# Final sums of a diffusion-block kernel: x1 of two token tiles through an identity product, all by halves of 512 columns, the last norm's weights loaded during the experts

## The chip, the cores and the metric

The kernel runs on one core of a Trainium2 chip, in one launch. The metric is the device time of one execution in microseconds; of several runs the median is taken. TensorE (PE) multiplies, VectorE (DVE) and ScalarE (ACT) work on tiles, GpSimd (POOL) does small vector steps and issues indirect and other DMAs, SyncE (SP) issues most of the weight DMAs.

## The reference, cut to what matters

The reference is one layer of a hybrid block (attention and a gated recurrence side by side), then a mixture of experts, then a final norm, over 512 tokens of 1024 channels:

```python
x = x + mod_lat[2] * mix_lat                       # x1 below
h_lat = rmsnorm(x, norm_ffn_g[l]) * (1 + mod_lat[4]) + mod_lat[3]
x = x + mod_lat[5] * moe_ffn(h_lat, ...)           # top 4 of 32 experts, D_EXPERT = 1024
return rmsnorm(x, final_norm_g)

def rmsnorm(x, g):
    y = x * rsqrt(mean(x * x, axis=-1, keepdims=True) + EPS)
    return y * g
```

An expert is an up product of 1024 by 2048 (gate and linear part interleaved), a clamped SwiGLU, and a down product of 1024 by 1024; each token's four expert outputs are weighted by a softmax of the router's four best values.

## The kernel before, in words

**Tokens.** The 512 tokens are four tiles of 128 rows. After the mixers, x1 (the stream after the first residual) lies in DRAM in three pieces `x1p`, of columns 0 to 511, 512 to 767 and 768 to 1023.

**Experts.** The 32 experts run one after the other, sorted so that the largest come first. Their weights come in chunks of 1 MB: eight of `w_gu` and four of `w_dn` each. `load_chunk` (L818) issues them from SyncE into 16 slots, through `next_chunk` (L1219), which gives back the slot of the chunk before and loads the next ones into free slots. `up` (L1257) multiplies the gathered rows of an expert with eight chunks, `glu` does the activation, `turned_acts` (L1278) transposes it, `down` (L1296) multiplies with four chunks, which this document calls its quarters, and scales the sums by the token's probability and the modulation `m5` into `yt` (L1305). `scatter` (L1309) adds `yt` to x1 in DRAM with indirect DMAs from POOL, for experts 0 to 30.

**The last expert.** Expert 31 is not scattered. Its rows in `yt` (64 slots, columns 0 to 511 on partitions 0 to 63, columns 512 to 1023 on partitions 64 to 127) are put in the place of their tokens by a product with a one-hot matrix `oh` of tokens by slots: for each token tile t two products (L1394), one per half of the columns, into PSUM. DVE adds the 1024 columns of PSUM to x1 of the tile (L1396). Then `finish_tile` (L1373) takes the sum of squares on ACT (Square with an accumulator, L1375; the profile shows the read of the accumulator as an instruction of its own), the reciprocal root on POOL (two steps, L125 and L126), scales by it and by the last norm's weights `gain` on DVE (L1377), and writes the tile out, tiles 0 to 2 from ACT's queue, tile 3 from SyncE's (L1378).

**What is loaded for the end.** After the last up product is in the program, `hold` takes five of the slots that were used last and are free: the first for `gain` (1024 weights, the same on all 128 partitions, loaded by SyncE at L1388), the others for x1 of tiles 0 to 3. `load_x2` (L1367) loads x1 from DRAM with twelve DMAs from POOL, three per tile, behind the scatters of expert 30. A slot that served the chunk k of the last up product can be written when that chunk's products are done: with five in `hold`, `gain` has chunk 6 and the tiles 0 to 3 chunks 5, 4, 3 and 2.

**PSUM.** There are eight banks of 512 columns: "gu" and "dn" are one tile each of three banks, "tp" is two tiles of one bank. Token tiles 0 and 2 use "gu", 1 and 3 use "dn"; a tile may be written when its last reader is done.

**Order.** The functions write a program order. A planner then orders the instructions of each engine: it follows a cost model and takes, of those whose inputs it believes to be ready, the one that is earliest in the program; instructions inside `tc.high_priority()` go ahead. It also sets every wait. Each engine then works through its queue in that order. The pool `y2k` has 18 buffers of 512 columns: during the experts they hold the transposed inputs and activations, three for `m5`, and short-lived tables.

**After the tiles.** From L1400 all engines load a count of experts with too many tokens. It is zero here, so the loop that would handle them, and finish the tiles again, is passed over.

Of the kernel before, what the change touches and what calls it, by code (L numbers as in the profile page):

```python
# [11 lines left out]
F32 = mybir.dt.float32  # L12
# [5 lines left out]
AF = mybir.ActivationFunctionType  # L18
OP = mybir.AluOpType
# [4 lines left out]
D = 1024  # L24
S = 512
# [3 lines left out]
NE = 32  # L29
# [17 lines left out]
NR = 3  # L47
# [32 lines left out]
def tile_block(ctx: ExitStack, tc: tile.TileContext, x, xc, cols, w_mod, b_mod, w_in, w_q_b, w_kv_b,  # L80
               w_out, g_ffn, w_r, b_r, w_gu, b_gu, w_dn, b_dn, g_fin, cst, rope, msk, out):
    nc = tc.nc
    V, A, G, PE, SP = nc.vector, nc.scalar, nc.gpsimd, nc.tensor, nc.sync
# [9 lines left out]
    ident = cs[:, K_ID:K_ID + 128]  # L93
# [22 lines left out]
    def y2k(dt, nm):  # L116
        return ypool.tile([128, S], dt, name=nm, tag="y2k")
# [55 lines left out]
    with tc.tile_pool(name="pa", bufs=1) as pa:  # L173
# [17 lines left out]
        for i in range(6):  # L191
            t = pa.tile([128, D], F32, name="xt", bufs=4)
            src = x[i * 128:(i + 1) * 128] if i < 4 else xc[(i - 4) * 128:(i - 3) * 128]
# [20 lines left out]
        for i in range(6):  # L214
            sq = pa.tile([128, D], BF16, name="sq")
# [3 lines left out]
            p = wide().rearrange("p a (k t) -> p (a k) t", t=128)  # L219
# [10 lines left out]
        for g in range(2):  # L230
            for which in (1, 0):

                pm = bank()[:, :128]
                for k in range(KD):
                    w = wms[8 * g + 4 * (1 - which) + k // 2]
                    for j in range(4):
                        PE.matmul(pm[32 * j:32 * j + 32], sc32[:, k], w[:, k % 2, j * 128:(j + 1) * 128],
                                  start=k == 0, stop=k == KD - 1)
# [9 lines left out]
                if which == 1:  # L248
                    gm = col[:, C_GM + 4 * g:C_GM + 4 * g + 4]
                    V.scalar_tensor_tensor(dst, dst, 1.0, gm[:, :, None].broadcast_to([128, 4, 2]),  # L250
                                           op0=OP.add, op1=OP.mult)
            for k in range(4 * g, 4 * g + 4):
                hf = pa.tile([128, T], F32, name="hf", bufs=2)
                for j, (a, b) in enumerate(((0, S), (S, T))):
                    V.tensor_scalar(hf[:, a:b], xnT[:, k, a:b], ac[:, k, j:j + 1], bc[:, k, j:j + 1],
                                    op0=OP.mult, op1=OP.add)
# [541 lines left out]
    def buffer(i, dt=F32):  # L798
        return pools[i].tile([128, 2 * D], dt, name=f"slot{i}")
# [72 lines left out]
    with tc.tile_pool(name="wo", bufs=2, side="right") as wo:  # L872
# [10 lines left out]
        for k in range(3, KD):  # L883
            t = buffer(k - 3, F32R).rearrange("p (a d) -> p a d", a=2)
            load_wo(k, t[:, 0], t[:, 1])
        rstack.close()
        early = ctx.enter_context(tc.tile_pool(name="sle", bufs=1))
# [204 lines left out]
    yt = piece(F32, 2)  # L1092
    glus = [piece(F32, i)[:, :NR * 256] for i in (3, 4)]

    free = deque(range(14, N_BUF))

    def borrow(dt=F32):

        i = free.popleft()
        free.append(i)  # L1100
        return buffer(i, dt)

    with tc.tile_pool(name="mo", bufs=2) as mo, tc.tile_pool(name="eps", bufs=2, space=PSUM) as eps:
# [115 lines left out]
        def next_chunk(key):  # L1219

            free.extend(taken)
            i, raw = raws.pop(key)
            taken[:] = [i]
            while n_loaded[0] < len(chunks) and free:
                load_chunk(free.popleft())
            return raw
# [66 lines left out]
                    V.tensor_copy(aT[1][:, 2:, b:b + 32], p[:, 2 * r:2 * r + 2, 96:])  # L1293
            return aT

        def down(e):  # L1296
            ps = sums(e, "dn")
            bias(ps, e, 256, 2 * D)
            for q in range(4):
                raw = next_chunk((e, "dn", q))  # L1300
                for j in range(2):
                    product(ps, e, aTs[e][q // 2][:, 2 * (q % 2) + j], raw[:, j * D:(j + 1) * D], 256, q + j == 4)
            big = CAPS[e] == CAP
            for r in rounds(e):
                V.scalar_tensor_tensor(yt[:, 256 * r:256 * r + 256], ps[:, r, :256],  # L1305
                                       prob[:, e, r * big:r * big + 1], (m5x if big else m5y)[r],
                                       op0=OP.mult, op1=OP.mult)
# [18 lines left out]
        for r in range(NR):  # L1326
            G.tensor_copy(m5x[r][:96], m5[:96, 256 * r:256 * r + 256])
            G.tensor_copy(m5x[r][96:], m5[96:, 768:])
        m5c = y2k(F32, "m5")
        m5y = [m5c[:, :256], m5c[:, 256:]]  # L1330
        for r in range(2):
# [24 lines left out]
                xTs[e + 1] = turned(xgs[(e + 1) % 2], CAPS[e + 1])  # L1356


        hold = [free.pop() for _ in range(5)]
        gain, xs = buffer(hold[0])[:, :D], []  # L1360

        def weighed(y, ps, pb):
            for n in range(2):
# [2 lines left out]

        def load_x2():  # L1367
            for t in range(4):
                xs.append(buffer(hold[1 + t])[:, :D])
                for a, b, x1 in x1p:  # L1370
                    G.dma_start(xs[t][:, a:b], x1[t * 128:(t + 1) * 128])

        def finish_tile(t, u):  # L1373
            sm = mo.tile([128, 4], F32, name="sm", bufs=4)
            A.activation(borrow()[:, :D], u, AF.Square, accum_out=sm[:, 0:1])  # L1375
            r = rstd_small(sm[:, 2:3], sm[:, 0:1], D, 1)
            v = V.scalar_tensor_tensor(u, u, sm[:, 2:3], gain, op0=OP.mult, op1=OP.mult).ins  # L1377
            o = (SP if t == 3 else A).dma_start(out[t * 128:(t + 1) * 128], u).ins  # L1378
            return r, v, o


# [3 lines left out]
            V.tensor_scalar(gf[:, t], gidx[:, NE - 1, 0:1], -128.0 * t, None, op0=OP.add)  # L1385
        V.tensor_tensor(oh, iota[:, None, :].broadcast_to([128, 4, 128]), gf.broadcast_to([128, 4, 128]), OP.is_equal)

        SP.dma_start(gain, bass.AP(tensor=g_fin.tensor, offset=g_fin.offset, ap=[[0, 128], [1, D]]))  # L1388
        load_x2()
        down(NE - 1)  # L1390
        for t in range(4):
            p = eps.tile([128, NR, S], F32, name=("gu", "dn")[t % 2], bufs=1)[:, :2]
            for n in range(2):
                PE.matmul(p[:, n], oh[64 * n:64 * n + 64, t], yt[64 * n:64 * n + 64, :S], start=True, stop=True)  # L1394
            with tc.high_priority():
                V.tensor_tensor(xs[t], xs[t], p.rearrange("p a b -> p (a b)"), OP.add)  # L1396
                last = finish_tile(t, xs[t])


        with tc.issue_after(last[0]), tc.issue_after(last[1]), tc.issue_after(last[2]):  # L1400
# [2 lines left out]
        with tc.For_i(0, n_any):  # L1403
            with tc.For_i(0, n_ov) as i:
                ev = nc.values_load(ov_e[0:1, ds(i, 1)], min_val=0, max_val=NE - 1)
                ex = nc.values_load(ov_x[0:1, ds(i, 1)], min_val=0, max_val=NE - 1)
                rk = mo.tile([128, 4, 1], F32, name="rk", bufs=1)
                V.tensor_tensor(rk, rankm[:, :, ds(ev, 1)], ov_r[:, None, ds(i, 1)].broadcast_to([128, 4, 1]), OP.subtract)
                pe = mo.tile([128, 4, 128], BF16, name="pe", bufs=1)
                V.tensor_tensor(pe, iota[:, None, :].broadcast_to([128, 4, 128]), rk.broadcast_to([128, 4, 128]),  # L1410
                                OP.is_equal)
                inf = mo.tile([128, 4, 8], BF16, name="inf", bufs=1)
                V.tensor_scalar(inf[:, :, None], info[:, :, ds(ev, 1), :], 1.0, None, op0=OP.mult)
                ps = eps.tile([128, 4, 128], F32, name="tp").rearrange("p a b -> p (a b)")
                for t in range(4):
                    PE.matmul(ps[:, :8], pe[:, t], inf[:, t], start=t == 0, stop=t == 3)
                gi = mo.tile([128, 1], I32, name="gi", bufs=1)
                pb = mo.tile([128, 1], F32, name="pb", bufs=1)
                slot_tables(mo, ps[:, :8], 1, gi, pb)
                selc = mo.tile([96, 128], BF16, name="selc", bufs=1)  # L1420
                V.tensor_scalar(selc, sel[:, ds(ev, 1)].to_broadcast([96, 128]), 1.0, None, op0=OP.mult)
                xg = xgs[0]
                gather(xg, gi)

                def in_turn(src):
                    h = y2k(F32, "oT")
                    p = eps.tile([128, 4, 128], F32, name="tp").rearrange("p a b -> p (a b)")
                    for k in range(4):
                        PE.transpose(p[:, k * 128:(k + 1) * 128], src[:, k * 128:(k + 1) * 128], ident)
                    V.tensor_copy(h, p)  # L1430
                    return h.rearrange("p (k s) -> p k s", s=128)

                def layer(ps, part, xT, w):
                    for n in range(2):
                        c0 = part * D + n * S
                        PE.matmul(ps[:, n], selc, bias_t[:, c0:c0 + S], start=True, stop=False)
                    for c in range(KD):
                        raw = borrow()[:, :D]
                        SP.dma_start(raw, w(c))
                        for n in range(2):  # L1440
                            PE.matmul(ps[:, n], xT[c // 4][:, c % 4], raw[:, n * S:(n + 1) * S],
                                      start=False, stop=c == KD - 1)

                xT = [in_turn(xg[:, a * S:(a + 1) * S]) for a in range(2)]
                aT = []
                for n in range(2):
                    ps = eps.tile([128, NR, S], F32, name="gu", bufs=1)[:, :2]
                    layer(ps, n, xT, lambda c: w_gu[ds(ex, 1), c * 128:(c + 1) * 128, n * D:(n + 1) * D]
                          .rearrange("e r c -> (e r) c"))
                    aT.append(in_turn(glu(ps, *(z[:, :S] for z in glus))))  # L1450
                ps = eps.tile([128, NR, S], F32, name="dn", bufs=1)[:, :2]
                layer(ps, 2, aT, lambda c: w_dn[ds(ex, 1), c * 128:(c + 1) * 128].rearrange("e r c -> (e r) c"))
                y = borrow()[:, :D]
                weighed(y, ps, pb)
                for a, b, x1 in x1p:
                    add_rows(x1, y[:, a:b], gi)
            scatter(NE - 1)
            del xs[:]
            load_x2()
            for t in range(4):  # L1460
                finish_tile(t, xs[t])


# [58 lines left out]
```

## Time and profile before

| | us |
|---|---|
| median of the runs shown | 1993.99 (1990.43, 1993.99, 1994.44) |
| profiled execution | 1993.45 |
| its span | 1991.5 |
| PE busy | 1855.6 (93%) |
| DVE busy | 816.8 (41%) |
| ACT busy | 430.4 (22%) |
| POOL busy | 277.8 (14%) |
| HBM read | 495.95 MB, 258 GB/s over the span |

The span is the time between the first and the last instruction of the profiled execution; all positions in this document are microseconds from its start. TensorE's granted clock is 0.986 of full speed over the span. The experts take about the second half, from 913 on, where the DMA engines move near 400 GB/s. The part that the change touches is the last 60 us, and one load early in the experts.

### The profile page before, as it was taken

The numbers are of one execution on the slowest core, as the hardware profiler recorded it, in microseconds if no ns is written. First come the engines' busy times: TensorE is split into PE (matmuls) and PEld (weight loads), VectorE is DVE, ScalarE is ACT, GpSimd is POOL, SyncE is SP. The second block draws the span as 40 slices with busy tenths as digits, with TensorE's granted clock in tenths as the row PEclk, the third lists the DMA queues.
The fourth block names the chain that finished last, engine by engine and source line by source line (L and its number), as shares of the span: only waits on it lengthen the run. The fifth ranks groups of instructions, "written<-read, shape, count | busy, mean of one in ns | idle before, by whom it ended". The sixth has DMA issues, their size and how long they took to land.

```text
span 1991.5 us, 40184 instructions
## 1 busy us (share of the span) xinstructions
PE 1855.6 (93%) x17276; PEld 1176.4 (59%) x17276; DVE 816.8 (41%) x1449; ACT 430.4 (22%) x717; POOL 277.8 (14%) x266
## 2 busy tenths in 40 slices
PE   5999999999999999998999999998899899988984
PEld 4999988998888788884355443333343334333431
DVE  5477877786757677755121111101110111010102
ACT  4233333333334554521000000000000000000001
POOL 1023000000000000012121221211221121212122
PEclk8999999999999999998999999999999999999998
DMA  9312434343121111369999999999999999999994
GB/s 301 98 56 84 137 118 121 99 140 85 33 77 55 44 38 53 91 259 371 346 396 395 394 404 391 393 398 406 388 399 398 399 388 396 394 403 386 402 402 160
DMA packets 164609, 512.68 MB, mean 257 GB/s; under 512 B 18640, under 2 KB 96370, under 8 KB 115276
## 3 DMA queue, kind: packets, MB, share of 16 engines
q1 hardware_dynamic: 149996, 487.99, 64.8%
q0 software_dynamic: 13856, 19.99, 4.4%
q8 instruction: 137, 2.24, 0.5%
q10 hardware_dynamic: 576, 2.10, 0.3%
q14 instruction: 44, 0.36, 0.1%
HBM read 495.95 MB, written 17.12 MB: 258 GB/s over the span
## 4 chain that ended last, share of the span: by engine, by line
PE 66%; DMA 28%; DVE 2%; issue 1%; ACT 1%; POOL 0%; SPq 0%; DVEq 0%; ACTq 0%; POOLq 0%
PE sc L282 24%; DMA slot<-in_w_gu 14%; PE gu L1255 14%; DMA slot<-in_w_dn 12%; PE dn L1255 7%; PE sc L688 3%; PE acc L434 3%; PE tp L709 1%; PE tp L1285 1%; PE sc L934 1%; PE acc L282 1%; PE sc L935 1%; PE sc L936 1%; DMA raw<-in_w_mod 1%; PE tp L1214 1%
## 5 line engine op out<-in xcount | busy, mean ns | idle before, releaser
L1255 PE MATMUL gu<-slot,xT 128*32 128x512 f32 x5120 | 579.2, 598 | 42.7 <-DMA slot<-in_w_gu 41.9
L282 PE MATMUL sc<-hh,part 128*128 128x384 f32 (+1 forms) x1472 | 404.6, 370 | 3.0 <-ACT part L120 3.0
L1255 PEld LDWEIGHTS gu<-slot,xT 128*32 128x32 f32 x5120 | 174.0, 110 | 391.3 <-issue 294.2
L1255 PE MATMUL dn<-slot,aT 128*32 128x256 f32 x5120 | 301.3, 382 | 10.9 <-DMA slot<-in_w_dn 10.1
L282 PEld LDWEIGHTS sc<-hh,part 128*128 128x128 f32 x1472 | 269.2, 190 | 34.6 <-issue 6.6
L1255 PEld LDWEIGHTS dn<-slot,aT 128*32 128x32 f32 x5120 | 157.0, 110 | 131.0 <-DMA slot<-in_w_dn 19.5
L1271 DVE TENSOR_SCALAR part<-gu 128x768 f32<-128x768 f32 (+1 forms) x32 | 26.4, 825 | 506.4 <-PE gu L1255 506.4
L282 PE MATMUL sc<-hl,part 128*128 128x384 f32 (+1 forms) x736 | 233.4, 365 | 0.0
L1274 ACT ACTIVATE part<-part 128x768 f32<-128x768 f32 (+1 forms) x32 | 23.6, 737 | 707.1 <-DVE part L1271 707.1
L1202 POOL DMA_INDIRECT x1d<-part,gidq x48 | 63.7, 1328 | 579.0 <-DVE part L1305 422.1
L282 PEld LDWEIGHTS sc<-hl,part 128*128 128x128 f32 x736 | 136.7, 189 | 11.2 <-issue 0.2
L121 DVE TENSOR_TENSOR part<-raw,part 128x1024 fp32r<-128x1024 f32 (+1 forms) x101 | 102.7, 1019 | 93.4 <-ACT part L120 93.3
L120 ACT ACTIVATE part<-raw 128x1024 fp32r<-128x1024 f32 (+1 forms) x101 | 89.4, 888 | 204.2 <-PE sc L282 146.8
L1305 DVE SCALAR_TENSOR_TENSOR part<-dn,prob,m 128x256 f32<-128x256 f32 x80 | 34.4, 479 | 237.4 <-PE dn L1255 224.8
L1202 POOL DMA_INDIRECT x1d<-part,gidx x77 | 108.3, 1407 | 86.3 <-DVE part L1305 60.4
L434 PE MATMUL acc<-qq,kc 128*128 128x128 f32 x448 | 63.4, 285 | 0.5 <-DVE qq L451 0.5
L434 PEld LDWEIGHTS acc<-qq,kc 128*128 128x128 f32 x448 | 60.9, 191 | 3.2 <-DVE qq L451 1.0
L430 ACT ACTIVATE kc<-kk 128x512 f32<-128x512 f32 x56 | 37.8, 675 | 108.8 <-PE acc L434 76.1
L441 DVE TENSOR_TENSOR kk<-kk,tt 128x768 f32<-128x768 f32 x56 | 59.0, 1054 | 0.0
L852 DVE TENSOR_TENSOR pe<-cs,rankm 128x384 bf16<-128x384 f32 x32 | 17.7, 553 | 98.6 <-PE tp L863 95.2
L451 DVE TENSOR_TENSOR qq<-qq,tt 128x256 f32<-128x256 f32 x112 | 47.2, 463 | 21.2 <-PE acc L434 21.0
L1196 POOL DMA_INDIRECT part<-h2d,gidx x31 | 32.3, 1042 | 161.5 <-PE tp L1214 125.2
(365 smaller groups left out, 2102.9 us busy)
## 6 DMA issues: line engine op xcount, KB each, us to landing
slot<-in_w_gu SPq DMA_DIRECT2D x256, 1024.0 KB
slot<-in_w_dn SPq DMA_DIRECT2D x128, 1024.0 KB
raw<-in_w_in SPq DMA_DIRECT2D x64, 512.0 KB
raw<-in_w_mod SPq DMA_DIRECT2D x48, 512.0 KB
raw<-in_w_q_b SPq DMA_DIRECT2D x12, 384.0 KB
xt<-in_x SPq DMA_DIRECT2D x8, 512.0 KB
raw<-in_w_out SPq DMA_DIRECT2D x8, 512.0 KB
raw<-in_w_kv_b SPq DMA_DIRECT2D x16, 128.0 KB
```

Source lines behind the costliest of these rows:

```text
L120: A.activation(hi, src, AF.Copy)
L121: V.tensor_tensor(lo, src, hi.bitcast(F32), OP.subtract)
L282: PE.matmul(ps[:, j, :b - a], w, x[:, a:b], start=first and n == 0, stop=last and n == 2)
L430: A.activation(kc, comb(kk, T, b, S), AF.Copy)
L434: PE.matmul(p[:, c], kc[:, c * 128:(c + 1) * 128], comb(qq, S, b, 128, c * 128), start=True, stop=True)
L441: V.tensor_tensor(kv_, kv_, mu, OP.mult)
L451: V.tensor_tensor(qv, qv, fv.broadcast_to([128, nb, b]), OP.mult)
L688: PE.matmul(ps[:, i, :HT], lhs, rhs[:, a:e], start=n == 0, stop=n == 4)
L1196: G.indirect_dma_start(out=xg, out_offset=None, in_=h2d, in_offset=bass.IndirectOffsetOnAxis(ap=idx, axis=0), bounds_check=S - 1, oob_is_e ...
L1202: G.indirect_dma_start(out=x1, out_offset=bass.IndirectOffsetOnAxis(ap=idx, axis=0), in_=y, in_offset=None, bounds_check=S - 1, oob_is_err ...
L1255: PE.matmul(ps[rows, r, :w], xT[:, slots], wt[:, cols_], start=False, stop=last)
L1305: V.scalar_tensor_tensor(yt[:, 256 * r:256 * r + 256], ps[:, r, :256], prob[:, e, r * big:r * big + 1], (m5x if big else m5y)[r], op0=OP.m ...
```

## The change

`down` gets a parameter `between`, a function that is called ahead of the products of the last quarter; for the last expert it is `early`. `early` writes, for tiles 0 and 1, a product of the identity with each half of the tile's x1 into PSUM (`begin`), as the first of two accumulating products; the one-hot product then adds to it, so that the sum of these tiles stands in PSUM and DVE's addition falls away. Tile 0 uses two banks of "gu", tile 1 the two "tp" tiles, tile 2 "dn" and tile 3 "gu". For tiles 2 and 3 DVE adds as before, by halves.

`finish_tile` works by halves of 512 columns: two Squares with two accumulators, an addition of them on POOL (one more step), the two steps of the root as before, and two scalings, from PSUM into the tile's buffer for tiles 0 and 1, in place for 2 and 3. The tile is written out with one DMA as before.

`gain` is two `y2k` buffers, loaded by POOL with two DMAs of 512 columns at the start of the experts, between the copies of `m5`; SyncE's load at the end falls away. `hold` is four slots: x1 of tiles 0 to 3 has the slots of chunks 6, 5, 4 and 3.

```diff
-        def down(e):
+        def down(e, between=None):
             ps = sums(e, "dn")
             bias(ps, e, 256, 2 * D)
             for q in range(4):
                 raw = next_chunk((e, "dn", q))
+                if between and q == 3:
+                    between()
                 for j in range(2):
...
+        gain = [y2k(F32, "gain") for _ in range(2)]
+        for n in range(2):
+            G.dma_start(gain[n], bass.AP(tensor=g_fin.tensor, offset=g_fin.offset + n * S, ap=[[0, 128], [1, S]]))
...
-        hold = [free.pop() for _ in range(5)]
-        gain, xs = buffer(hold[0])[:, :D], []
+        hold, xs = [free.pop() for _ in range(4)], []
...
-                xs.append(buffer(hold[1 + t])[:, :D])
+                xs.append(buffer(hold[t])[:, :D])
...
-        def finish_tile(t, u):
+        def column_halves(a):
+            return [a[:, n * S:(n + 1) * S] for n in range(2)]
+
+        def finish_tile(t, src):
             sm = mo.tile([128, 4], F32, name="sm", bufs=4)
-            A.activation(borrow()[:, :D], u, AF.Square, accum_out=sm[:, 0:1])
+            sq, u = column_halves(borrow()), column_halves(xs[t])
+            for n in range(2):
+                A.activation(sq[n], src[n], AF.Square, accum_out=sm[:, n:n + 1])
+            G.tensor_tensor(sm[:, 0:1], sm[:, 0:1], sm[:, 1:2], OP.add)
             r = rstd_small(sm[:, 2:3], sm[:, 0:1], D, 1)
-            v = V.scalar_tensor_tensor(u, u, sm[:, 2:3], gain, op0=OP.mult, op1=OP.mult).ins
-            o = (SP if t == 3 else A).dma_start(out[t * 128:(t + 1) * 128], u).ins
+            for n in range(2):
+                v = V.scalar_tensor_tensor(u[n], src[n], sm[:, 2:3], gain[n], op0=OP.mult, op1=OP.mult).ins
+            o = (SP if t == 3 else A).dma_start(out[t * 128:(t + 1) * 128], xs[t]).ins
             return r, v, o
...
-        SP.dma_start(gain, bass.AP(tensor=g_fin.tensor, offset=g_fin.offset, ap=[[0, 128], [1, D]]))
         load_x2()
-        down(NE - 1)
+        ends = {}
+
+        def begin(t):
+            if t == 1:
+                ends[t] = [eps.tile([128, 4, 128], F32, name="tp").rearrange("p a b -> p (a b)") for _ in range(2)]
+            else:
+                p = eps.tile([128, NR, S], F32, name="dn" if t == 2 else "gu", bufs=1)
+                ends[t] = [p[:, n] for n in range(2)]
+            for n, x1 in enumerate(column_halves(xs[t])):
+                if t < 2:
+                    PE.matmul(ends[t][n], ident, x1, start=True, stop=False)
+
+        def early():
+            begin(0)
+            begin(1)
+
+        down(NE - 1, early)
         for t in range(4):
-            p = eps.tile([128, NR, S], F32, name=("gu", "dn")[t % 2], bufs=1)[:, :2]
+            if t > 1:
+                begin(t)
             for n in range(2):
-                PE.matmul(p[:, n], oh[64 * n:64 * n + 64, t], yt[64 * n:64 * n + 64, :S], start=True, stop=True)
+                PE.matmul(ends[t][n], oh[64 * n:64 * n + 64, t], yt[64 * n:64 * n + 64, :S], start=t > 1, stop=True)
             with tc.high_priority():
-                V.tensor_tensor(xs[t], xs[t], p.rearrange("p a b -> p (a b)"), OP.add)
-                last = finish_tile(t, xs[t])
+                src = ends[t]
+                if t > 1:
+                    src = column_halves(xs[t])
+                    for n in range(2):
+                        V.tensor_tensor(src[n], src[n], ends[t][n], OP.add)
+                last = finish_tile(t, src)
```

## Rows read from the trace of the kernel before

**Rows 1.** Chain of waits in order of time, tail: start us, us, what.

```profile
1940.23 25.17 DMA slot<-in_w_dn
...
1965.44 1.98 PE dn L1255 x32
...
1968.47 1.14 PE gu L1394 x4
...
1969.63 1.23 DVE slot L1396
...
1980.52 1.28 DVE slot L1377
```

**Rows 2.** Timeline of TensorE: start us, us, what, [idle before <- releaser].

```profile
1955.54 0.74 PE L1285 MATMUL tp<-cs,part 128*128 128x128 f32 x4 [2.22 <-DVE part L1275]
...
1962.05 1.93 PE L1255 MATMUL dn<-slot,aT 128*32 128x256 f32 x32 [1.52 <-DMA slot<-in_w_dn]
1965.44 1.93 PE L1255 MATMUL dn<-slot,aT 128*32 128x256 f32 x32 [1.46 <-DMA slot<-in_w_dn]
...
1969.40 1.05 PE L1394 MATMUL dn<-part,oh 64*128 64x512 f32 x4
```

**Rows 3.** Timeline of the other engines after the last weights.

```profile
1970.94 1.06 ACT L1375 ACTIVATE slot<-slot 128x1024 f32<-128x1024 f32 x1 [13.90 <-DVE slot L1396]
1971.90 0.18 ACT L1375 ACTIVATION_READ_ACCUMULATOR slot<-slot 128x1 f32 x1
...
1973.07 1.28 DVE L1377 SCALAR_TENSOR_TENSOR slot<-slot,sm,slot 128x1024 f32<-128x1024 f32 x1 [1.08 <-POOL sm L126]
...
1978.57 1.28 POOL L125 TENSOR_SCALAR sm<-sm 128x1 f32<-128x1 f32 x1
...
1981.84 0.35 SPq L1378 DMA_DIRECT2D out<-slot  x1
```

**Rows 4.** Lines L1371, L1375 (ns min/median/max, starts); SyncE's waits (us, times, longest).

```profile
L1371 POOL DMA_DIRECT2D slot<-x1d x12: 536/536/630, 1947.6 to 1958.7; - x12
...
L1375 ACTq EVENT_SEMAPHORE  x11: 17/38/11569, 1956.4 to 1975.5; - x11
...
SPq L1378 <- DMA slot<-x1d: 4.5, 1, 4.5
```

**Rows 5.** DMA queues, 1961 to 1965.4, then 1965.4 to 1968.1: packets, MB, share.

```profile
q1 hardware_dynamic: 36, 0.20, 11.0%
q0 software_dynamic: 45, 0.13, 7.6%
...
q1 hardware_dynamic: 12, 0.04, 3.9%
q0 software_dynamic: 15, 0.04, 3.6%
```

**Rows 6.** Stretches: us, PE, PEld, DVE, ACT, POOL busy, clock, DMA share, GB/s.

```profile
945.00:955.00 10.00, 10.00 (x88) 3.05 (x84) 0.00 (x0) 0.70 (x2) 0.97 (x1) 0.86 0.77 249
...
1372.20:1374.40 2.20, 0.10 (x8) 0.06 (x8) 0.00 (x0) 0.00 (x0) 0.00 (x0) 1.00 1.00 421
1374.40:1377.80 3.40, 3.40 (x20) 0.84 (x24) 0.00 (x0) 0.00 (x0) 0.00 (x0) 0.50 1.00 410
...
1936.70:1941.00 4.30, 4.26 (x28) 1.28 (x32) 0.00 (x0) 0.00 (x0) 3.69 (x3) 0.50 1.02 389
...
1955.50:1958.00 2.50, 1.93 (x28) 1.31 (x32) 0.58 (x1) 0.66 (x2) 1.07 (x2) 1.00 0.94 346
```

**Rows 7.** Groups by form: busy us, mean ns, idle before.

```profile
L343 PE MATMUL tp<-raw,ones 128*1 128x512 f32 x16 | 7.5, 591 | 0.0
...
L491 ACT ACTIVATE sq<-acc 128x512 f32<-128x512 f32 x8 | 4.8, 598 | 22.7 <-PE acc L488 22.7
...
L1271 DVE TENSOR_SCALAR part<-gu 128x512 f32<-128x512 f32 x16 | 11.1, 692 | 277.9 <-PE gu L1255 277.9
...
L1275 DVE SCALAR_TENSOR_TENSOR part<-part,part 128x512 f32<-128x512 f32 x16 | 11.1, 693 | 1.8
```

More of the change, by code (lines that the diff above doesn't have):

```diff
@@ L1460, in tile_block @@
             for t in range(4):
-                finish_tile(t, xs[t])
+                finish_tile(t, column_halves(xs[t]))
 def _consts():
```

## The prediction

> **What bounds the kernel now.** I read the chain of waits in order of time first, since the change sits in the last 60 us. There the reader sees one transfer, the last w_dn chunk, on the path for 25.17 us until 1965.40; then 1.98 us of products, a step of 1 us in which `yt` is scaled, 1.14 us for the first one-hot product, 1.23 us for the first sum, and at the end the scaling by the gain at 1980.52 [rows 1]. The timeline of TensorE shows the same from the engine: the third quarter of the down products ends at 1963.98, TensorE stands 1.46 us, and the fourth ends at 1967.38 [rows 2]. Then the timeline of the others: a Square of 1.06 us per tile, its read of 0.18 us, two POOL steps, a scaling of 1.28 us, and the last output issued at 1981.84 [rows 3]. So there are two stretches: up to 1967.38 the weights bound it, and from there 14.46 us to the last output are a chain through DVE, ACT and POOL. What follows the last output (9.7 us to the span's end) begins with its landing and, I take it, moves with it.
>
> Last I looked at when x1 arrives, because the new products read it. POOL issues the twelve loads from 1947.6 to 1958.7. SyncE, which writes tile 3's output, is free of its wait for x1 after 4.5 us, while POOL still issues. ACT's waits ahead of the Squares are the opposite: the first begins at 1956.4, the longest lasts 11.57 us, so it ends at 1968.0 or later, and tile 0's is the first Square [rows 4]. So the loads go out in the order tile 3, 2, 1, 0: tile 3's buffer is the first to be freed. Tile 0's x1 lands about 1968.0, after the last weights, and today nobody minds, as its sum comes at 1969.63. The DMA view agrees. From 1961 to 1965.4 the two queues fill 18.6% of 16 engines, which is three of them at work on what is late, the last weights and x1; after 1965.4 the x1 queue (q0) still moves 15 packets beside 12 of q1, by then the gain load [rows 5].
>
> **The change, part by part.**
>
> *The gain load* leaves SyncE for POOL, early in the experts, as two halves. It adds 512 KB to the weight stream there. The DMA engines are 0.77 busy in 945 to 955 [rows 6], which is 2.3 us to spare, and 512 KB at the 410 GB/s of a full stretch [rows 6] is an estimated 1.3 us. So 0; if that cover were gone, +1.3. It takes two more of the 18 `y2k` buffers; with three for m5 and eight for the operands of two experts none runs out: 0. POOL's two issues, 0.54 us each like L1371's [rows 4], lie beside TensorE's work: 0. At the end, 12 of 27 packets are gone [rows 5], so tile 0's x1 comes about 1 us sooner: 1967.0 for 1968.0, and its first half, the load issued first, about 1966.0. Bounds: no sooner at all, or by the whole 2.6 us since the last weights.
>
> *The buffers.* `hold` has four, not five: tile 0 takes the slot of chunk 6 in place of chunk 5. Tile 0's loads go last, up to 1958.7, and TensorE is through with every up product 2.22 us before 1955.54 [rows 2]: 0. The order tile 3 to tile 0 stays.
>
> *The identity products.* Two per tile, 128 rows by 512 columns in f32. An f32 product is two passes: eight products of L343 are 16 instructions [rows 7]. Four passes of L1394 (two products side by side) take the 0.93 us from 1968.47 to 1969.40 [rows 1, 2]; a product of full height has none beside it, so it takes about 0.9 us: 4 x 0.9 = 3.6 us. Bounds: 0.59 us each (one pass of L343, the other hidden), 2.4 us, and 1.2 us each, 4.7 us. They stand ahead of the fourth quarter in TensorE's queue: behind the waiting product are the 32 instructions of that quarter, and for these wait `yt`, all four one-hot products and everything after. Tile 0: first half 1966.0 to 1966.9, second half 1967.0 to 1967.9, tile 1 (landed by then) to 1969.7; the fourth quarter, 1.93 us [rows 2], to 1971.65. That is 4.3 us later than 1967.38. Had x1 been there, the cost would be 3.6 - 1.46 = 2.1 us.
>
> *The sums.* For tiles 0 and 1 the sum on DVE goes (1.23 us, on the path for tile 0). Square is by halves, 0.598 us each from PSUM [rows 7], with a second read of 0.18: 1.34 for 1.15 us. POOL adds the two halves, one more step of 0.2 us and its gap: 1.1 for 0.86. From the end of the down products: 1.09 to the one-hot product, 1.14, 1.34, 1.1 and gaps of 0.2: tile 0's scaling starts at 4.9 us instead of 5.69 (1973.07 - 1967.38) [rows 3].
>
> The DVE steps by halves cost what the wholes cost: 0.693 us for 128x512 [rows 7] with about 0.61 between starts, 1.3 for 1.28. The scalings of tiles 0 and 1 read PSUM. Here L1271 (from PSUM) and L1275 (from SBUF) measure 692 and 693 ns [rows 7], so I take no extra. [...]
>
> *From there to the last output.* Tile 3 now needs the banks that hold tile 0's sum until tile 0 is scaled (before, the banks of tile 1, until it was added). So in a row: scaling of tile 0 from 4.9, 1.3; product of tile 3, 1.2; its sum, 1.3; Square to the read, 0.9 after the sum's end; POOL, 1.15; scaling, 1.3: 12.05 us. In the holes DVE must place tile 2's sum and the scalings of tiles 1 and 2, and a scaling with both inputs in SBUF holds POOL: L125 took 1.28 us beside one [rows 3]. So up to 1.1 more; I take 12.8. Against 14.46 that gives 1.7 us back (between 1.3 and 2.4).
>
> **The sum:** +4.3 - 1.7 = +2.6 us. On the profiled execution, 1993.45 (1.95 of it outside the span), that is 1996.0; the median of the runs shown, 1993.99, lies 0.5 above, so 1996.5.
>
> **Rivals.**
>
> *Identity products behind the fourth quarter.* The order is set by the planner, which takes what it believes to be ready. For it: it turned the x1 loads round by readiness, and tile 0's is the last. Against: in the program they come first. Then the quarter ends at 1967.38 as now, tile 0's products run to 1969.2, the one-hot product starts 0.7 us later than now (2.5 if tile 1's go ahead too), and with 1.7 back the net is -1.0 to +0.8: about 1994.
>
> *They stand further ahead*, at the wait for the third quarter, if the planner sees a hole there. Then both quarters, 3.9 us, follow tile 0's x1: 1.9 us more, +4.5, 1998.5. For it: TensorE also stands 1.5 us before that quarter. Against: by the program they come later.
>
> *TensorE at its lower clock (the other side).* Place: the stand from 1963.98 to tile 0's x1, near 2.0 us, is longer than the 1.46 of today. [...] Against: the stand of 2.22 us before 1955.54 [rows 2] is followed by 1.00 [rows 6], as are today's of 1.5 us, 1.93 us of products each [rows 2]. If it falls, the 3.6 + 1.93 + 1.14 us behind it run at half: 1.7 us lost for 3.4 us of it, 3.3 us if all of it falls. The net is +4.3 to +5.9: 1998 to 2000. It turns a loss within the measurement into a clear one from 2.8 us at half. [...]
>
> *The change does not do what it says:* x1 of tiles 0 and 1 is loaded first, so the products do not wait. Then +2.1 - 1.7 = +0.4, 1994.5. Against it is the order read from rows 4.
>
> **How the numbers follow.** Chances: forecast 0.40; behind the quarter 0.27; further ahead 0.10; lower clock 0.15; x1 early 0.08. The runs shown differ by 4 us, about 0.2% (4.0 us), which is also what a measurement here can tell from no change. Slower by over that: nearly all of the clock, most of "further ahead", and the part of the forecast in which x1 comes no sooner: 0.26. Faster by over that has no case in the sum; 0.07 for what I overlook and for the runs' spread. The same: 0.67. Range: from 1991.5 (products behind, 2.4 us back, and the spread) to 2000.5 (clock at half).
>
> **What the profile after would show.** TensorE idle after the third quarter until about 1966, eight identity passes, the fourth quarter's end near 1971.6, granted clock 1.0 throughout; no wait for the gain; POOL's steps of tiles 0 and 1 at 0.19 us, as their scalings read PSUM; the last output 12 to 13 us after the fourth quarter. Wrong if the identity passes start right at 1964 (x1 early), stand behind the quarter, or if the last weights land over 1 us away from 1965.4 (gain not hidden).

## The result, and the profile after

The changed kernel takes 2005.21 us in the median of ten runs (1996.60 to 2007.09), the kernel before 1993.82 in ten on the same chip. The ratio is 1.0055, with a 95% interval of 1.0038 to 1.0072: 11.0 us slower (7.6 to 14.4). The profiled execution took 2002.65 us, with a span of 2000.8. The forecast was 1996.5, its range ended at 2000.5, and the chance given to slower was 0.26.

The timeline of TensorE answers to [rows 2]: start and length in us, and in brackets the idle time ahead of a row and what ended it. In all that follows a stand is such idle time of TensorE. L1412 are the identity products, L1285 the transposes of the last activations, L1255 the down products, L1423 the one-hot products.

```profile
1963.31 2.05 PE L1412 MATMUL gu<-slot,cs 128*128 128x512 f32 x2 [12.09 <-DMA slot<-x1d]
1965.15 1.06 PE L1285 MATMUL tp<-cs,part 128*128 128x128 f32 x4
1966.00 1.76 PE L1412 MATMUL gu<-slot,cs 128*128 128x512 f32 x2
1967.70 5.39 PE L1255 MATMUL dn<-slot,aT 128*32 128x256 f32 x96
1973.01 1.99 PE L1412 MATMUL tp<-slot,cs 128*128 128x512 f32 x4
1974.93 1.93 PE L1255 MATMUL dn<-slot,aT 128*32 128x256 f32 x32
1977.86 1.13 PE L1423 MATMUL gu<-part,oh 64*128 64x512 f32 x4 [1.00 <-DVE part L1307]
...
1983.08 1.13 PE L1423 MATMUL gu<-part,oh 64*128 64x512 f32 x4 [2.37 <-DVE slot L1389]
```

What matters is the place of the first L1412. Tile 0's first half stands not ahead of the fourth quarter but ahead of everything that TensorE does for the last expert after its up products: the transposes, and with them all four quarters, whose 96 + 32 instructions come only afterwards. It reads tile 0's x1, the last group to land, and TensorE stands 12.09 us for it, from 1951.22 to 1963.31. By then the weights of three quarters are there: they run through in 5.39 us with no wait between them, where the third quarter waited 1.52 us before, as the fourth did 1.46 [rows 2]. Tile 1's products stand where the forecast had all of them, ahead of the fourth quarter.

Of the waits of TensorE from 1945 to 1985 (us, times, longest) one outweighs all others. SyncE's wait for tile 3's x1, the last line, is longer than in [rows 4], 15.7 us for 4.5, but this is no part of the loss: SyncE no longer has the gain load to issue first, and the wait ends at 1953.5, 2.3 us behind the up products, where before it ended at 1956.2, 2.9 behind them.

```profile
PE gu L1412 <- DMA slot<-x1d: 12.1, 1, 12.1
PE gu L1423 <- DVE slot L1389: 2.4, 1, 2.4
PE gu L1423 <- DVE part L1307: 1.0, 1, 1.0
...
SPq L1390 <- DMA slot<-x1d: 15.7, 1, 15.7
```

The stretches (us; PE, PEld, DVE, ACT and POOL busy; granted clock, DMA share, GB/s) answer to [rows 6]. TensorE's granted clock goes from 1.00 to 0.50 while it stands, and is 0.50 over the 4.3 us behind the stand too:

```profile
1951.20:1953.80 2.60, 0.02 (x4) 0.00 (x0) 2.39 (x4) 0.63 (x1) 1.08 (x3) 1.00 0.77 279
1953.80:1963.20 9.40, 0.00 (x0) 0.00 (x0) 0.19 (x1) 0.00 (x0) 1.06 (x2) 0.50 0.35 121
1963.20:1967.50 4.30, 4.19 (x8) 1.92 (x8) 0.00 (x0) 0.66 (x2) 0.00 (x0) 0.50 0.00 0
1967.50:1977.00 9.50, 9.36 (x133) 4.63 (x132) 0.07 (x1) 0.00 (x0) 0.00 (x0) 1.00 0.02 3
```

The DMA share shows the other side: the weights had all but landed while TensorE still stood. From 1961 to 1965.4, where before 36 packets of weights moved (q1) [rows 5], 4 do, beside the last of x1 (q0); the up products had ended 2.1 us earlier than before, which accounts for a part of this:

```profile
q0 software_dynamic: 34, 0.09, 5.6%
q1 hardware_dynamic: 4, 0.02, 0.9%
```

The loads of x1 themselves (POOL's issues of L1375; ns min/median/max, first and last start) are as in [rows 4], 2.7 to 2.9 us earlier; the up products end 2.1 us earlier in this execution (1951.22 for 1953.32):

```profile
L1375 POOL DMA_DIRECT2D slot<-x1d x12: 536/543/621, 1944.9 to 1955.8; - x12
```

The chain of waits, which began with the weights in [rows 1], breaks off at a piece without a releaser, "issue", that lasts until the first Square; what it names behind that is the tail:

```profile
1966.90 12.18 issue
...
1983.59 1.28 DVE slot L1429 x2
...
1986.79 0.71 ACT slot L1385 x2
1987.57 0.76 POOL sm L1386
```

VectorE's timeline behind the down products, and the last output, answer to [rows 3]:

```profile
1976.93 0.88 DVE L1307 SCALAR_TENSOR_TENSOR part<-dn,prob,m 128x256 f32<-128x256 f32 x2 [22.94 <-PE dn L1255]
1981.61 1.41 DVE L1389 SCALAR_TENSOR_TENSOR slot<-gu,sm,gain 128x512 f32<-128x512 f32 x2 [3.80 <-POOL sm L126]
1982.93 0.74 DVE L1389 SCALAR_TENSOR_TENSOR slot<-tp,sm,gain 128x512 f32<-128x512 f32 x1
1983.59 1.28 DVE L1429 TENSOR_TENSOR slot<-slot,dn 128x512 f32<-128x512 f32 x2
1984.79 0.75 DVE L1389 SCALAR_TENSOR_TENSOR slot<-tp,sm,gain 128x512 f32<-128x512 f32 x1
1985.45 1.28 DVE L1429 TENSOR_TENSOR slot<-slot,gu 128x512 f32<-128x512 f32 x2
1986.85 1.41 DVE L1389 SCALAR_TENSOR_TENSOR slot<-slot,sm,gain 128x512 f32<-128x512 f32 x2
1989.26 1.41 DVE L1389 SCALAR_TENSOR_TENSOR slot<-slot,sm,gain 128x512 f32<-128x512 f32 x2 [1.00 <-POOL sm L126]
...
1990.70 0.35 SPq L1390 DMA_DIRECT2D out<-slot  x1
```

The down products end at 1976.86 and the last output is issued 13.84 us later (before 14.46, forecast 12.8). VectorE stands 3.80 us ahead of tile 0's scaling, although tile 2's one-hot product was done at 1980.70: tile 2's sum (L1429, 1983.59) comes behind that scaling in the queue.

### The profile page after: what moved, and what is told of

Read it like the earlier page. It is cut to its first block, busy times and chain, and to the rows that moved or that the text cites. A ratio compares the mean times of both kernels' runs of the same rounds, so it can differ in the third digit from the quotient of the medians.

```text
span 2000.8 us, 40202 instructions
## 1 busy us (share of the span) xinstructions
PE 1859.0 (93%) x17284; PEld 1179.6 (59%) x17284; DVE 814.7 (41%) x1453; ACT 430.4 (22%) x725; POOL 277.6 (14%) x272
## 5 line engine op out<-in xcount | busy, mean ns | idle before, releaser
L1255 PE MATMUL gu<-slot,xT 128*32 128x512 f32 x5120 | 577.9, 597 | 42.9 <-DMA slot<-in_w_gu 42.5
L1255 PEld LDWEIGHTS gu<-slot,xT 128*32 128x32 f32 x5120 | 174.8, 110 | 390.1 <-issue 295.6
L1255 PE MATMUL dn<-slot,aT 128*32 128x256 f32 x5120 | 301.7, 383 | 7.9 <-DMA slot<-in_w_dn 7.6
L1255 PEld LDWEIGHTS dn<-slot,aT 128*32 128x32 f32 x5120 | 157.7, 110 | 128.9 <-DMA slot<-in_w_dn 18.1
```

Source lines behind the costliest of these rows:

```text
L1255: PE.matmul(ps[rows, r, :w], xT[:, slots], wt[:, cols_], start=False, stop=last)
```

## The experiments

The theory, T1: the loss is TensorE's in-order queue standing on the x1 that lands last, ahead of the down products, and the low clock behind that stand. Rivals: R1, the early load of the norm's weights or its two buffers slow the experts; R2, the halves make the tail longer; R3, the products themselves; R4, the clock falls for another reason than the stand.

Executions of one kernel differ by some 10 us (1986.59 to 1998.21 for the ten of the kernel before), in part in when the weights come: the last up product ends between 1949.2 and 1954.3 in the twelve profiles. So I read from each profile three stretches that depend little on that: A from the end of the last up products to the end of the last down products, B from there to the issue of the last output, C from there to the span's end. Beside the difference of their sum to the kernel before stands what the repeated runs gave, worked out from the ratio and the median of before on the same chip.

```
                      A      B      C     sum   diff   by the runs (95%)
before             14.06  14.46   9.66  38.18
after              25.64  13.84  10.10  49.58  +11.4  +11.0 (+7.6 to +14.4)
e1_behind          14.06  16.43  10.28  40.77   +2.6   +1.2 (-1.0 to  +3.2)
e2_x1_first        14.46  13.86   9.93  38.25   +0.1   +1.0 (-1.6 to  +3.8)
e3_no_identity     14.07  14.76  10.81  39.64   +1.5   +2.4 (-0.2 to  +5.0)
e4_no_wait         14.36  13.84  10.31  38.51   +0.3    0.0 (-2.2 to  +2.0)
e5_between         19.49  13.84  10.33  43.66   +5.5   +4.2 (+1.6 to  +6.6)
e6_t0_third        22.85  13.85  10.33  47.03   +8.9  +10.2 (+7.4 to +12.7)
e7_sums_first      14.32  11.70  10.05  36.07   -2.1   -1.0 (-3.2 to  +1.0)
e8_gain_late       14.28  13.84   9.52  37.64   -0.5   +0.2 (-1.8 to  +2.4)
e9_sums_ahead      13.92  11.43  11.42  36.77   -1.4   -0.8 (-3.8 to  +2.0)
e10_ahead_late     14.07  11.43  10.14  35.64   -2.5   -2.6 (-5.6 to  +0.4)
```

**e1_behind: the identity products behind the last down product.**

```diff
-        down(NE - 1, early)
+        with tc.issue_after(down(NE - 1)):   # down returns its last product
+            early()
...
```

> Identity products of both tiles issued only behind the last product of the fourth quarter; all else as in the changed kernel. T1 (the loss is TensorE's queue standing on tile 0's x1, at half clock, ahead of the down products): the twelve down transposes and products run as their weights land, ending about 1965 to 1967.5 of the span, 4 products of 0.6 to 0.9 us follow, and the tail is about 14 to 15 us: -1.5 to +3 against the kernel before, clock back at full in the tail. R1 (gain load or its two buffers in the experts) and R2 (the halves of the tail): the loss stays, +8 to +12. R3 (the products' own time): +2.5 to +4 with the tail longer by just these 3.6 us.

Measured: ratio 1.0006 (0.9995 to 1.0016), so the loss is gone with everything else of the change still in it, which goes against R1 and R2 as its cause. A is 14.06, as before to the hundredth. B is 16.43: the 3.6 us of products now stand between the last quarter and the one-hot products, 2.6 us more than in the changed kernel.

**e2_x1_first: tile 0's x1 loaded first.**

```diff
-                xs.append(buffer(hold[t])[:, :D])
+                xs.append(buffer(hold[3 - t])[:, :D])
```

> Tile 0's x1 takes the buffer that comes free first, so it is loaded first and lands at about 1956 instead of 1963.5; TensorE's order is that of the changed kernel. T1: TensorE stands only until about 1954 to 1957, the first three quarters run as they land, the stand now falls on tile 1's x1 ahead of the fourth quarter or nowhere: 0 to +5. R1, R2: unchanged, +8 to +12. R3: +2.5 to +4 of products alone whatever the order of the loads, the clock as in the changed kernel.

Measured: ratio 1.0005 (0.9992 to 1.0019). One index takes the loss away, with TensorE's order untouched. Its timeline shows the first identity products 1.46 us behind the up products, where they wait for VectorE to empty the bank, no longer for x1:

```profile
1952.01 1.10 PE L1412 MATMUL gu<-slot,cs 128*128 128x512 f32 x2 [1.46 <-DVE part L1272]
1952.94 0.63 PE L1285 MATMUL tp<-cs,part 128*128 128x128 f32 x4
1953.50 1.10 PE L1412 MATMUL gu<-slot,cs 128*128 128x512 f32 x2
1954.53 3.66 PE L1255 MATMUL dn<-slot,aT 128*32 128x256 f32 x64
1959.30 1.93 PE L1255 MATMUL dn<-slot,aT 128*32 128x256 f32 x32 [1.11 <-DMA slot<-in_w_dn]
```

Beside the changed kernel's rows this splits its A, 11.18 us longer than here: 10.63 more of standing (12.09 for 1.46), 1.87 more from the first identity product to the first down product (4.39 for 2.52, the clock at half), and 1.32 less in the three quarters up to tile 1's products (5.31 for 6.63, as their weights had landed).

**e3_no_identity: the change without its identity products**, all four sums on VectorE by halves.

```diff
-        down(NE - 1, early)
+        down(NE - 1)
...
-                src = ends[t]
-                if t > 1:
-                    ...
+                src = column_halves(xs[t])
+                for n in range(2):
+                    V.tensor_tensor(src[n], src[n], p[:, n], OP.add)
```

> The change without its products with the identity: all four tiles are added on VectorE, by halves, the norm's weights still loaded during the experts and scaling still by halves. T1: nothing stands ahead of the down products: -2 to +1.5. R1, R2: the loss is still there, +6 to +12. R3: the loss goes, as under T1; this run does not tell the two apart.

Measured: ratio 1.0012 (0.9999 to 1.0025). The loss is gone, but the middle, +2.4, lies above what T1 had expected. A is that of before, B 0.3 longer: the halves alone gain nothing, and the 0.3 us that they cost are a small part of the loss that R2 would have to explain.

**e4_no_wait: the same products in the same place, without the wait.** They read a tensor that has long been in SBUF, so x1 is left out of tiles 0 and 1.

```diff
-            for n, x1 in enumerate(column_halves(xs[t])):
+            for n, x1 in enumerate(column_halves(m5)):
```

> The identity products read a tensor that has been in SBUF since before the experts in place of x1, which leaves x1 out of tiles 0 and 1; their number, size and place in TensorE's order stay. T1: the work without the wait costs its 3.6 us at most, and half of it falls into idle time before the weights land: -1 to +3. R3 (the products themselves, or their place in the order without any wait): +8 to +12. R4 (the clock falls for another reason than the standing): granted clock 0.5 from about 1954 to 1967 all the same and +4 to +8.

Measured: ratio 1.0000 (0.9989 to 1.0010). Number, size and place of the products cost nothing that shows (A is 0.3 longer, and the runs leave room for 2 us), against R3; and over the instructions that the changed kernel runs at 0.5 the clock stays at 1.00, against R4:

```profile
1951.60:1953.10 1.50, 0.01 (x1) 0.05 (x1) 1.34 (x3) 0.63 (x1) 0.94 (x3) 1.00 0.84 281
1953.10:1957.40 4.30, 4.30 (x44) 2.30 (x48) 1.24 (x2) 0.66 (x2) 1.52 (x4) 1.00 0.78 275
```

**e5_between: the products held where the prediction had them.**

```diff
                 if between and q == 3:
-                    between()
+                    with tc.issue_after(done):            # third quarter's last product
+                        after.append(between())           # fourth quarter behind these
...
```

> The identity products held to the place that the prediction gave them: all four behind the third quarter's last down product and ahead of the fourth quarter's first; the loads of x1 stay as in the changed kernel, tile 0 last. T1: what is left of the loss is the prediction's own sum with the tail as now measured (13.84 for the forecast 12.8): 4 products by 0.9 us at most, less the wait for the fourth quarter's weights, so about +1.5 to +4.5 against the kernel before, clock at full. R1, R2: the loss of the changed kernel stays, +8 to +12. If the forecast's place was right all along and something else is slow: also +8 to +12.

Measured: ratio 1.0021 (1.0008 to 1.0033), +4.2 us. The interval holds the forecast's +2.6, but also the +4.3 to +5.9 of the prediction's rival with the lower clock, so the profile has to decide. The wait is as forecast: TensorE waits 2.10 us for tile 0's x1 (forecast near 2.0):

```profile
1965.20 3.31 PE L1418 MATMUL gu<-slot,cs 128*128 128x512 f32 x4 [2.10 <-DMA slot<-x1d]
1968.31 2.26 PE L1418 MATMUL tp<-slot,cs 128*128 128x512 f32 x4
1970.50 1.93 PE L1255 MATMUL dn<-slot,aT 128*32 128x256 f32 x32
```

The eight passes take 5.30 us from start to start instead of 3.6, for here the clock does fall behind the stand, as that rival had it and as neither the forecast nor T1 did:

```profile
1965.20:1968.30 3.10, 3.10 (x4) 1.22 (x5) 0.00 (x0) 0.00 (x0) 0.00 (x0) 0.57 0.00 0
1968.30:1970.50 2.20, 2.20 (x6) 0.72 (x4) 0.00 (x0) 0.00 (x0) 0.00 (x0) 0.83 0.00 0
```

So in its own place the prediction's working holds for the wait, but not for the clock, and its tail of 12.8 is 13.84 here too.

**e6_t0_third: half a dose.** The changed kernel with tile 0's x1 third and tile 1's last.

```diff
-                xs.append(buffer(hold[t])[:, :D])
+                xs.append(buffer(hold[(1, 0, 2, 3)[t]])[:, :D])
```

> The changed kernel with the buffers of tiles 0 and 1 exchanged, so that tile 0's x1 is loaded third and tile 1's last; the order of TensorE stays. T1: the stand ahead of the down products ends when the third group of x1 lands, about 2.5 to 3.5 us sooner than the fourth, and nothing more is won behind it, since tile 1's products then wait for the last group only if that is later than the third quarter: +5 to +9 against the kernel before. R1 to R3: as the changed kernel, +8 to +12.

Measured: ratio 1.0051 (1.0037 to 1.0064). In the profile the stand is 9.27 us, 2.82 less than 12.09, and A 2.79 shorter, one for one as T1 has it. The stretches put it at +8.9, inside the range given; the five runs put it at +10.2, above that range and not apart from the changed kernel's. That the loss follows the landing rests on the profile and on e2, not on these times.

```profile
1958.44 2.05 PE L1412 MATMUL gu<-slot,cs 128*128 128x512 f32 x2 [9.27 <-DMA slot<-x1d]
```

**e7_sums_first: e2, and VectorE's sums ahead of the scalings**, with tile 3 in tile 2's bank.

```diff
...
+        with tc.issue_after(spread(2)), tc.high_priority():   # tile 2's sum
+            finish_tile(0, ends[0])
+        with tc.issue_after(spread(3)), tc.high_priority():   # tile 3's sum
+            for t in range(1, 4):
+                last = finish_tile(t, ends[t])
```

> Tile 0's x1 first, as in e2_x1_first, and in VectorE's order tile 2's sum ahead of tile 0's scaling and tile 3's ahead of tile 1's, with tile 3's products in the bank of tile 2. If the 3.80 us in which VectorE stood idle ahead of tile 0's scaling are what kept the tail from coming down as forecast: from the end of the down products to the last output 12.0 to 12.6 us in place of 13.84, and -2.5 to +0.5 against the kernel before. If the tail is held by the squares and the root of the last tile: 13.5 to 14 us and +0 to +3.5, as e2_x1_first.

Measured: ratio 0.9995 (0.9984 to 1.0005), and B is 11.70: the tail comes down by 2.14 us, more than expected. This rests on the profile: the runs put e7 1.2 us under e8 below, which has e2's order and was timed on the same chip, with intervals that overlap, and neither apart from the kernel before. VectorE's timeline now runs from the first sum to the end without a gap:

```profile
1967.65 1.28 DVE L1429 TENSOR_TENSOR slot<-slot,dn 128x512 f32<-128x512 f32 x2 [2.95 <-PE dn L1423]
1968.85 1.40 DVE L1389 SCALAR_TENSOR_TENSOR slot<-gu,sm,gain 128x512 f32<-128x512 f32 x2
1970.17 1.28 DVE L1429 TENSOR_TENSOR slot<-slot,dn 128x512 f32<-128x512 f32 x2
1971.37 1.40 DVE L1389 SCALAR_TENSOR_TENSOR slot<-tp,sm,gain 128x512 f32<-128x512 f32 x2
1972.69 2.73 DVE L1389 SCALAR_TENSOR_TENSOR slot<-slot,sm,gain 128x512 f32<-128x512 f32 x4
```

**e8_gain_late: e2 with the norm's weights loaded behind the experts again**, into a fifth buffer.

```diff
-        gain = [y2k(F32, "gain") for _ in range(2)]
-        ...
+        SP.dma_start(late, bass.AP(tensor=g_fin.tensor, offset=g_fin.offset, ap=[[0, 128], [1, D]]))
```

> As e2_x1_first, but the norm's weights are loaded behind the experts, into a fifth buffer, as in the kernel before. If the early load costs nothing (the prediction's step): the time of e2_x1_first within 1.5 us, and the groups of x1 land about 1 us later, which nothing waits for here. R1 (early load and its buffers slow the experts' weights): 1.5 to 3 us faster than e2_x1_first.

Measured: ratio 1.0001 (0.9991 to 1.0012), 0.8 us below e2 with intervals that overlap. No cost of the early load is shown; these times leave room for one of up to about 4 us. The profiles show none either: from expert 0's first up product to expert 31's last, the nine with the early load take 1037.3 to 1041.2 us (mean 1039.0), the three with the late one 1036.7 to 1040.6 (mean 1039.2).

**e9_sums_ahead and e10_ahead_late: what the runs point to.** Tile 0's x1 first, tile 1's products ahead of the third quarter, one-hot products in the order of tiles 2, 0, 1, 3, both sums ahead of all scalings; e10 loads the norm's weights late.

```diff
...
+                    if between and q == 2:
+                        with tc.issue_after(done):
+                            held.enter_context(tc.issue_after(begin(1)))
...
+        added = spread(2)
+        spread(0)
+        with tc.issue_after(added):
+            spread(1)
+            added = spread(3)
+        with tc.issue_after(added), tc.high_priority():
+            for t in (0, 2, 1, 3):
+                last = finish_tile(t, ends[t])
```

> A version that uses what the first eight runs showed: tile 0's x1 loaded first and its products as planned around the transposes, tile 1's products ahead of the third quarter (not of the fourth), the one-hot products in the order of tiles 2, 0, 1, 3, both sums of VectorE ahead of all scalings. T1 with the tail as counted in VectorE's queue: 0.4 us less ahead of the fourth quarter than e7_sums_first, the tail 11.0 to 11.6 us for 11.70; against the kernel before -4 to -1. If tile 1's products now stand on their x1 ahead of the third quarter: +0 to +2. If the tail is held by the roots on POOL and not by VectorE: as e7_sums_first, -2.5 to +0.5.

> As e9_sums_ahead, but with the norm's weights loaded behind the experts and behind x1, into a fifth buffer. If the early load costs nothing: as e9_sums_ahead within 1.5 us. R1: 1.5 to 3 us faster. If the late load still takes something from the last weights of the experts: 0.5 to 2 us slower.

Measured: 0.9996 (0.9981 to 1.0010) and 0.9987 (0.9972 to 1.0002). Both have A within 0.14 of before and B of 11.43, 3.0 us under the kernel before. In e9 1.8 us of that come back behind the last output (C 11.42), in e10 0.5. Both beat the changed kernel; that e10 beats the kernel before its interval does not quite show, and e9's -0.8 lies just short of the -4 to -1 that was expected.

## Why the prediction was wrong

**The step that failed** is the place of the identity products: "They stand ahead of the fourth quarter in TensorE's queue." Tile 0's stood ahead of the transposes and of all four quarters. I had read the order of the program as that of the queue. The point to ask was from when on they could be issued: they need no down product, only x1 and a free bank, and the bank of tile 0 is free as soon as VectorE has read the up sums, as e2 and e4 show (1.46 and 1.50 us behind the up products, ended by L1272). With the stand moved there, the prediction's own numbers give most of the loss: the first half of tile 0's x1, forecast for 1966.0, lands 12.7 us behind the up products (1953.32), and behind it come 3.6 us of identity products, 0.7 of transposes and 7.6 of down products, together 24.6 where A was 14.1, so +10.5, less what the tail gives back. Measured, A is 11.6 longer: the half came 0.6 us sooner than that (12.1 for 12.7), and the clock at half cost 1.9 (e2).

**The rival "further ahead"** named the mechanism, with a chance of 0.10, but looked one wait up, at the third quarter (+4.5), and so priced 3.9 us of products behind x1, where it was all 7.6 us, the transposes and the clock.

**The identity products.** Eight passes at 0.9 us a pair: rows of x4 take 1.98 to 1.99 us, so right to 0.1 a product. By themselves they make A 0.3 us longer (e4), since most of them fit into waits of TensorE: within A 5.7 us before, 2.6 in e4.

**x1 about 1 us sooner** with the gain out of the way: right. The x1 queue (q0) moves its last data 13.7 to 13.9 us behind the up products in the three profiles with the late gain load, and 12.0 to 12.7 in the nine with the early one, so 1.0 to 1.9 sooner.

**The gain load's cover** was read from the wrong place. POOL issues the load at 921.8, where the DMA share is 1.01 in the kernel before and 1.02 in the changed one (from 920 to 925), and not in 945 to 955, where the prediction found room. That it costs nothing was therefore not shown by the row given for it, though no run shows a cost (e8).

```profile
921.84 1.35 POOL L1333 DMA_DIRECT2D gain<-in_g_fin  x2
```

**The lower clock.** The forecast had 1.0 throughout; the rival was right as a mechanism, in the changed kernel behind a stand of 12.09 us (0.50) and in e5 behind 2.10 (0.57). The 3.4 us for which it has the clock at half are the length of the row from 1374.40, at 0.50 behind a stand of 2.10 us [rows 6]. But the rows also show a stand without a fall: 2.22 us before and 1.00 behind it [rows 2, 6].

**The tail**, forecast 12.8, was 13.84. Tile 0's scaling came 4.75 us behind the down products (forecast 4.9), tile 3's one-hot product 6.22 (6.2). Then the term "in the holes" failed: tile 2's sum and half of tile 1's scaling stood ahead of tile 3's sum and delayed it by 1.2 us, and POOL's first step for tile 3 took 0.75 us beside a scaling that reads SBUF alone, for 0.19 otherwise. So of the 1.7 us that the tail was to give back, 0.6 came. The forecast had tile 2's sum in a hole of VectorE's; e7 puts it there, and B is 11.70.

```profile
1981.59 0.19 POOL L1386 TENSOR_TENSOR sm<-sm 128x1 f32<-128x1 f32 x1
...
1987.57 0.75 POOL L1386 TENSOR_TENSOR sm<-sm 128x1 f32<-128x1 f32 x1 [0.75 <-ACT slot L1385]
```

**The halves** cost 1.41 us for two scalings, not 1.3, whatever they read: on line L1389 (ns min/median/max) the sources in SBUF, then in PSUM, differ by 3 ns.

```profile
L1389 DVE SCALAR_TENSOR_TENSOR slot<-slot,sm,gain x4: 743/747/751, 1986.9 to 1989.9; 128x512 f32<-128x512 f32 x4
...
L1389 DVE SCALAR_TENSOR_TENSOR slot<-tp,sm,gain x2: 743/744/746, 1982.9 to 1984.8; 128x512 f32<-128x512 f32 x2
```

So the PSUM source costs nothing more in these rows, as the prediction took it.

**Right:** no wait for the gain; POOL's addition and first root step of tiles 0 and 1 at 0.18 to 0.19 us, of which tile 1's lie beside a scaling that reads PSUM (the second root step takes 0.55 to 0.58); the x1 of tile 0 last. **Left open:** whether the early load of the gain takes something from the weights that these runs are too coarse to show.

## What to carry to other kernels

Before a product with an early operand and a late one is added to an in-order queue, work out from when on the program allows it to be issued, and price the stand from there: everything behind it in the queue waits for the late operand, here 12.09 us. If an engine is to consume what a set of loads brings, put the load that it needs first at the front of them: here one index was worth 10 us. When a change removes work from a chain, look whether its queue order lets the rest move up; in the profile, moving two sums ahead of the scalings (with tile 3's products in tile 2's bank) took 2.1 us off B, where replacing two others by identity products had taken off 0.9 (e3 against the changed kernel).

## What was not expected of the hardware

A stand of the same length does not always bring the clock down. Behind the 2.2 us before the transposes the granted clock was 1.00 in the kernel before [rows 6], but 0.60 in e1 over the 3.1 us from 1956.9, behind 2.21 us, 0.72 in e3 over the 5 us from 1956.4, behind 2.21, and 0.66 in e5 from 1955 to 1960, behind 2.23:

```profile
1956.90:1960.00 3.10, 3.10 (x36) 1.69 (x40) 0.00 (x0) 0.19 (x1) 0.67 (x2) 0.60 0.60 201
```

In e1 it cost nothing, since the fourth quarter's weights came later anyway, after a wait of 1.47 us (A 14.06 in both). The end of the span, too, moves by itself: from the issue of the last output it took 9.5 to 11.4 us in twelve profiles, most in e9.
